# The long sequence's gates as a stage of block products between Fourier mixing and retention, the short sequence's gates as filler

## The chip, the cores and the metric

The kernel runs on one core of one Trainium2 chip. The metric is the device time of one execution in microseconds (us); of several runs the median is given. The chip has a matrix engine (TensorE, PE in the profile, with its weight loads as PEld), VectorE (DVE), ScalarE (ACT), GpSimd (POOL), and SyncE (SP), whose queue issues most of the transfers between the device's memory (HBM) and the on-chip memory. Products accumulate in eight banks (`bank`) that DVE and ACT read out.

## The reference

One encoder layer with the same weights over two requests, one of 512 tokens and one of 1024, model width 1024:

```python
u = rms_norm(x, norm1_g)
f, q, k, v, g_ret, g_a, g_b = split(u @ w_in)       # 512, 512, 512, 1024, 1024, 1024, 1024 columns
branch_a = fourier_mix(f) @ w_four_proj             # 4 groups of 128: fft2 over tokens and channels, real part
branch_b = (group_norm(bidirectional_retention(q, k, v)) * silu(g_ret)) @ w_ret_proj
x = x + (sigmoid(g_a) * branch_a + sigmoid(g_b) * branch_b) @ w_out
x = x + (gelu(conv3(h_gate)) * h_val) @ w_down      # h_gate, h_val = split(rms_norm(x, norm2_g) @ w_up), 2816 each
y = rms_norm(x, final_norm_g)
```

Retention has 8 heads (keys of 64, values of 128), runs in chunks of 128 tokens in both directions with a decay per head, and rotates q and k.

## The kernel before

**Layout.** Activations lie with the channels on the 128 partitions: tile `x[t, k]` holds channels 128k to 128k+127 (k = 0 to 7) of 512 tokens. t=0 is the short sequence, t=1 and t=2 the long one. Every float32 product is made of three matmuls of rounded halves (`mm3`, L110 to L112): high by high, low by high, high by low. `split` makes the halves: ACT copies the high one (L74), DVE subtracts for the low one (L75). `slab` (L93) loads 128x1024 weights through SP into `wr` and splits them into `wh` and `wl`. A projection of 128 output channels and 512 tokens takes 24 matmuls of 128x512 (`proj_steps`).

**The norm.** `Prep` loads x (`fetch`, L187), makes u = x * g as halves (`scale`, L195 on ACT, L196 on DVE), without 1/rms. Squares come from ACT or POOL (`SumSq`); `cols` sums them over the partitions on PE (L130), DVE adds (L133), POOL raises to the power -1/2 (L134); `rows` spreads that over the partitions for a row per token (`rrow`). The factor is applied later: by `rrow` on the gates, per token on the Fourier channel DFT (L255, L256) and on q, k, v (L530). So no projection waits for the norm.

**Stages.** (1) Projection of f for t=0, 1, 2 (`f_proj`) with `channel_dft` (L249) and `sequence_dft` of the short sequence between; (2) channel and sequence DFT of the long one; (3) a loop over 8 output blocks n that multiplies the Fourier result `pq` with `w_four_proj`, then makes gate g_a of the three t (`gate`, L310: times `rrow` on DVE, sigmoid on ACT), multiplies it with the branch (L491) and stores the result (`ma`, L492); (4) retention over four head pairs: per pair 12 chunks of q, k, v (128 tokens by 512 columns, 24 matmuls each), then six g_ret gates of 24 matmuls, each with one POOL product (L683), while `sides` do the chunks' other steps on PE's gaps, the states and group norm (`ret_states`, L624 to L635) and the multiplication with g_ret (`ret_store`); (5) gates g_b for n=1 to 7 (`gb_main`), beside which the last pair's side work and the splitting of retention's results run; n=0 has run as a filler in the long sequence DFT; (6) merge (g_a part plus g_b times retention's projection), `w_out`, the up and down projections and the last norm. The stages from the merge on already compute pairs of 512-token halves as 2x2 blocks with seven products in place of eight (`w_ops`, `quad`, `quads`): a job is 7 products of 12 matmuls, 84.

**Order.** Code order gives each instruction's rank on its engine, and every engine and every queue runs in its order; an instruction waits for the semaphores of what it needs and for the space of its output. SP waits with a transfer for its source or its destination, and what is behind it waits too. The tiles u live from the norm to the last g_b gate. Line numbers here are those of the profile before.

Of the kernel before, what the change touches and what calls it, by code (L numbers as in the profile page):

```python
# [14 lines left out]
P = 128  # L15
# [9 lines left out]
SL_F, SL_GA, SL_GRET, SL_QKV, SL_GB = 0, 4, 12, 20, 36  # L25
SL_RP, SL_WO, SL_DL = 44, 52, 60
N_SLABS = 62
# [8 lines left out]
def emit(ctx, tc, x, wsl, wup, wdq, wd0, wfour, tab, cst, rcst, vec, out):  # L36
# [4 lines left out]
    uctx, wctx = ExitStack(), ExitStack()  # L41
    upool = uctx.enter_context(tc.tile_pool(name="u", bufs=24))
# [25 lines left out]
    x2_d = [[spill(f"xx{n}_{t}") for t in range(3)] for n in range(KD)]  # L68

    def utile(kind, dtype=F32R):  # L70
        return upool.tile([P, TC], dtype, name=kind, tag=kind)
# [5 lines left out]
    state = {"ww": (1152, 1032)}  # L77
# [5 lines left out]
    def wtiles():  # L83
        wpool = state["w"]
        wide, cols = state["ww"]
        r = wpool.tile([P, wide], F32, name="wr", tag="wr", bufs=2)
        state["turn"] += 1
        pool, n = (state["wx"], 1) if state["wx"] and state["turn"] % 5 == 4 or state["turn"] < 0 else (wpool, 4)
        return (r, *(pool.tile([P, cols], F32R, name=x, tag=x, bufs=n) for x in ("wl", "wh")))
# [70 lines left out]
    state["w"] = wctx.enter_context(tc.tile_pool(name="w", bufs=4, reuse_waits="tile"))  # L160
    bctx = ExitStack()
    rc = bctx.enter_context(tc.tile_pool(name="rc", bufs=1, reuse_waits="tile"))
    state.update(wx=bctx.enter_context(tc.tile_pool(name="wx", bufs=1, reuse_waits="tile")), turn=-1)

    fctx = ExitStack()
    pqp = fctx.enter_context(tc.tile_pool(name="pq", bufs=1, side="right", reuse_waits="tile"))
    f1ctx = ExitStack()
    fp = f1ctx.enter_context(tc.tile_pool(name="f1", bufs=13, side="right", reuse_waits="tile"))

    state["tmp"] = fp, "f2", 13  # L170
    u = [None] * 3
    rcol, rrow = [None] * 3, [None] * 3

    class Prep:
        def __init__(self, t):
            self.t = t
            self.ss = SumSq(rc.tile([P, R_END], F32, name="rs", tag="rs")[:, :TC] if t == 0 else None, t == 2)
            self.xs = []
            u[t] = ([], [])
# [10 lines left out]
        def scale(self):  # L190
            k = len(u[self.t][0])
            xs = self.xs[k]
            g = vc[:, V_G1 + k:V_G1 + k + 1]
            h, l = utile("uh"), utile("ul")
            nc.scalar.activation(h, xs, AF.Identity, scale=g)  # L195
            nc.vector.scalar_tensor_tensor(l, xs, g, h.bitcast(F32), op0=ALU.mult, op1=ALU.subtract)  # L196
            u[self.t][0].append(h)
            u[self.t][1].append(l)

        def square(self, k):  # L200
            self.ss.add(self.xs[k], self.t == 1 and k % 2 == 1)
            self.xs[k] = None
# [4 lines left out]
        def rows(self):  # L207
            ps = rstd_rows(rcol[self.t])
            rrow[self.t] = rc.tile([P, TC], F32, name=f"rrow{self.t}")
            nc.scalar.copy(rrow[self.t], ps)  # L210

# [24 lines left out]
    def channel_dft(si, pr):  # L236
        c0, ncs, t0, nt = SEQS[si]
        zt = []
        for c2 in range(ncs // 2):
# [11 lines left out]
            for j in range(2):  # L251
                c = 2 * c2 + j
                b = slice(j * 256, (j + 1) * 256)
                r = rcol[t0 + c // 4][:, c % 4:c % 4 + 1]
# [53 lines left out]
    def gate(pool, tag, ps, t, bufs=None):  # L308
        sg = pool.tile([P, TC], F32, name="sg", tag=tag, bufs=bufs)
        nc.vector.tensor_tensor(sg, ps, rrow[t], op=ALU.mult)  # L310
        nc.scalar.activation(sg, sg, AF.Sigmoid)
        return sg

    def gb_main(ns, pool, tag, bufs=None):
        for n in ns:
            wgb = wslab(SL_GB + n)
            for t in range(3):
                ps = bank()
                for _ in proj_steps(ps, wgb, u[t]):
                    yield  # L320
                sg = gate(pool, tag, ps, t, bufs)
                nc.scalar.dma_start(sb_d[n][t], sg)
                yield

# [3 lines left out]
    for k in range(4):  # L328
# [3 lines left out]
        preps[0].scale()  # L332
# [5 lines left out]
    for k in range(4):  # L338
        preps[0].scale()
# [3 lines left out]
    for k in range(KD):  # L343
        preps[0].square(k)
    fps = [bank() for _ in range(4)]
# [3 lines left out]
    preps[0].cols()  # L349
    for g in range(4):  # L350
        f_evac(0, g, fps[g])
    for k in range(KD):
        preps[1].scale()
        preps[1].square(k)

# [11 lines left out]
    for k in range(KD):  # L367
        preps[2].fetch()
    f_proj(1, 0)
    z00 = channel_dft(0, 0)  # L370
    f_proj(1, 1)
    z01 = channel_dft(0, 1)
    preps[1].cols()
    for k in range(KD):
        preps[2].scale()
    for i, _ in enumerate(sequence_dft(0, {0: z00, 1: z01})):
        preps[2].square(2 * i)
        preps[2].square(2 * i + 1)
    f_proj(2, 0)
# [10 lines left out]
    f_proj(2, 1)  # L390
    preps[2].cols()
# [17 lines left out]
    rs = rc.tile([P, R_END], F32, name="rs", tag="rs")  # L409
    nc.sync.dma_start(rs, rcst)  # L410

    decD, decT = {}, {}

    def decay_d(hp):
        D = rc.tile([P, 2, P], F32, name="D", tag="D", bufs=4)
# [11 lines left out]
    def decay_t(hp):  # L427
        TD = rc.tile([P, 2, P], F32, name="TD", tag="TD", bufs=2)
# [10 lines left out]
    for hp in range(4):  # L439
        decay_d(hp)  # L440
# [4 lines left out]
    state["turn"] = -1  # L445
    for q in preps:
        q.rows()
    z11 = channel_dft(1, 1)
    fill = gb_main(range(1), fp, "f2", 13)
    next(fill)  # L450
    for _ in sequence_dft(1, {1: z11}):
        next(fill, None)
    list(fill)
    f1ctx.close()

# [869 lines left out]
```

## Time and profile before

| | |
|---|---|
| runs: median (lowest to highest), us | 2282.02 (2279.92 to 2282.39), 3 runs |
| profiled execution, us | 2279.94 |
| its span, us | 2277.8 |
| busy in the span: PE, DVE, ACT, POOL | 98%, 65%, 37%, 15% |
| mean granted clock of PE | 0.991 |
| moved by DMA | 273.30 MB, 120 GB/s on the mean |

The profile is of one execution, whose own time is 2.1 us longer than its span. A row of a stretch gives for each engine its busy time in it, with the count of instructions, then PE's granted clock, the share of time that the DMA engines were busy, and what they moved. A row of a group gives line, engine, operation, output and inputs, count, then busy time, mean ns of one, and the idle time just ahead of it with what ended that. In a row of the timeline stand start, duration and the instruction, and in brackets how long the engine had been idle and what released it.

### The profile page before, as it was taken

Reading aid. Unit: us, or ns where it says so; the run is one execution under the profiler, and the core shown is the slowest. Engines: PE = TensorE matmul, PEld = TensorE weight load, DVE = VectorE, ACT = ScalarE, POOL = GpSimd, SP = SyncE. Lnnn points to the kernel's source line nnn. Section 1 sums busy time; section 2 is a strip of 40 time slices with the busy share of each in tenths; the row PEclk is TensorE's granted clock in tenths of the full one; section 3 lists DMA queues with packets and bytes.
Section 4 is the critical chain, followed back from the end, with each engine's and each line's share of the span. In section 5 each row is a group of like instructions: output and inputs, shape, how many; then the busy total and the mean of one; then the engine's idle time right before and its main releaser. Section 6 shows DMA issues by size and latency. Waiting matters only on the chain. (4 is left out here: it accounts for less than half of the span.)

```text
span 2277.8 us, 29367 instructions
## 1 busy us (share of the span) xinstructions
PE 2228.0 (98%) x11294; PEld 1866.6 (82%) x11294; DVE 1474.6 (65%) x2555; ACT 848.5 (37%) x1373; POOL 345.8 (15%) x184
## 2 busy tenths in 40 slices
PE   8899999999999999999999999999989999999997
PEld 6788888888888888878887788888867878999986
DVE  7453434656556462255678886767689888999744
ACT  6251222223121221133334444434453446666413
POOL 2799601111212120010120000000000000000001
PEclk9999999999999999999999999999999999999999
DMA  5252220111102012276756452323265455333462
GB/s 190 66 167 86 94 84 1 47 38 38 47 17 68 1 56 79 74 243 224 226 180 226 147 191 94 110 93 116 84 226 176 153 203 195 101 104 112 166 208 70
DMA packets 103531, 273.30 MB, mean 120 GB/s; under 512 B 11488, under 2 KB 14816, under 8 KB 97760
## 3 DMA queue, kind: packets, MB, share of 16 engines
q1 hardware_dynamic: 99936, 265.15, 35.1%
q10 hardware_dynamic: 3456, 6.29, 0.7%
q8 instruction: 88, 1.44, 0.3%
q14 instruction: 51, 0.42, 0.1%
HBM read 208.22 MB, written 63.18 MB: 119 GB/s over the span
## 5 line engine op out<-in xcount | busy, mean ns | idle before, releaser
L110 PE MATMUL bank<-op,wh 128*128 128x512 f32 (+1 forms) x1320 | 462.0, 352 | 8.0 <-DVE y L1096 4.2
L111 PE MATMUL bank<-op,wl 128*128 128x512 f32 (+1 forms) x1320 | 463.2, 351 | 1.1 <-DVE wl L75 1.1
L112 PE MATMUL bank<-op,wh 128*128 128x512 f32 (+1 forms) x1320 | 461.6, 350 | 1.1 <-DVE op L75 1.1
L75 DVE TENSOR_TENSOR wl<-wr,wh 128x1024 fp32r<-128x1024 f32 (+5 forms) x210 | 250.3, 1193 | 163.5 <-ACT wh L74 161.7
L74 ACT CAST wh<-wr 128x1024 fp32r<-128x1024 f32 (+5 forms) x210 | 204.8, 977 | 325.1 <-PE bank L112 220.7
L110 PEld LDWEIGHTS bank<-op,wh 128*128 128x128 f32 x1320 | 250.0, 189 | 48.3 <-DVE y L1096 5.2
L112 PEld LDWEIGHTS bank<-op,wh 128*128 128x128 f32 x1320 | 250.4, 190 | 37.6 <-DVE op L75 2.0
L111 PEld LDWEIGHTS bank<-op,wl 128*128 128x128 f32 x1320 | 250.3, 190 | 36.4 <-DVE wl L75 1.6
L110 PE MATMUL bank<-uh,wh 128*128 128x512 f32 x672 | 271.5, 404 | 5.2 <-ACT wh L74 5.2
L112 PE MATMUL bank<-ul,wh 128*128 128x512 f32 x672 | 266.0, 396 | 0.0
L111 PE MATMUL bank<-uh,wl 128*128 128x512 f32 x672 | 265.9, 396 | 0.0
L134 POOL TENSOR_TENSOR nr<-nv,mhalf 128x4 f32<-128x4 f32 (+1 forms) x10 | 12.9, 1285 | 1105.7 <-DVE nv L133 1075.8
L425 POOL TENSOR_TENSOR D<-two,D 128x64 f32<-128x64 f32 x16 | 170.2, 10667 | 0.0
L74 ACT CAST wh<-wt 128x1024 fp32r<-128x1024 f32 (+2 forms) x120 | 117.3, 977 | 135.9 <-PE bank L112 123.9
L110 PE MATMUL bank<-wh,uh 128*128 128x512 f32 x384 | 166.6, 434 | 0.0
L110 PEld LDWEIGHTS bank<-uh,wh 128*128 128x128 f32 x672 | 126.8, 189 | 32.1 <-ACT wh L74 5.2
L111 PE MATMUL bank<-wh,ul 128*128 128x512 f32 x384 | 151.4, 394 | 0.0
L112 PE MATMUL bank<-wl,uh 128*128 128x512 f32 x384 | 151.0, 393 | 0.0
L112 PEld LDWEIGHTS bank<-ul,wh 128*128 128x128 f32 x672 | 126.6, 188 | 29.4
L111 PEld LDWEIGHTS bank<-uh,wl 128*128 128x128 f32 x672 | 126.8, 189 | 27.7 <-DVE wl L75 0.8
L310 DVE TENSOR_TENSOR sg<-bank,rrow 128x512 f32<-128x512 f32 x48 | 33.2, 691 | 165.5 <-PE bank L112 165.5
L75 DVE TENSOR_TENSOR wl<-wt,wh 128x1024 fp32r<-128x1024 f32 (+2 forms) x120 | 135.6, 1130 | 6.5 <-ACT wh L74 6.3
(233 smaller groups left out, 4108.5 us busy)
## 6 DMA issues: line engine op xcount, KB each, us to landing
wr<-wsl SPq DMA_DIRECT2D x92, 512.0 KB, 3.9
wr<-wup SPq DMA_DIRECT2D x44, 1024.0 KB, 4.9
xs<-x SPq DMA_DIRECT2D x48, 256.0 KB, 4.2
wr<-tab SPq DMA_DIRECT2D x18, 516.0 KB, 3.7
wr<-wdq SPq DMA_DIRECT2D x12, 768.0 KB, 4.2
wr<-wd SPq DMA_DIRECT2D x16, 512.0 KB, 3.9
sb<-sg ACTq DMA_DIRECT2D x24, 256.0 KB, 2.0
ma<-sg SPq DMA_DIRECT2D x24, 256.0 KB, 2.0
```

The costliest lines, as they stand in the source:

```text
L74: nc.scalar.copy(h, src)
L75: nc.vector.tensor_tensor(l, src, h.bitcast(F32), op=ALU.subtract)
L110: nc.tensor.matmul(o, lh, rh, start=first, stop=False, skip_group_check=go_on)
L111: nc.tensor.matmul(o, ll, rh, start=False, stop=False, skip_group_check=go_on)
L112: nc.tensor.matmul(o, lh, rl, start=False, stop=last, skip_group_check=go_on)
L134: nc.gpsimd.tensor_tensor(r, v, mhalf[:, 0:n], op=ALU.pow)
L310: nc.vector.tensor_tensor(sg, ps, rrow[t], op=ALU.mult)
L425: nc.gpsimd.tensor_tensor(D[:, m], two.broadcast_to([P, 64]), D[:, m], op=ALU.pow)
```

## The change

**The long sequence's gates.** The three gates of t=1 and t=2 become 12 block jobs (`gate_job`) of 84 matmuls, run by the same `quads` that the up stage uses, in a stage of their own between Fourier and retention: 1008 matmuls in place of 1152. Eight jobs give g_a and g_b for n, four give g_ret for two n. Each loads 128x2048 weights (`wg`) and, for the first eight, the branch.
- The jobs need four sums of the operands u (S1 to S4, k = 0 to 3). `sums` makes them on DVE in the front, splits them and stores them in HBM (`s_d`); 32 loads of 256 KB bring them back (`sop`) at the gate stage's start. The branch of t=1, 2 is stored too (`br_d`, 8 x 512 KB), and the finished gates go to HBM.
- Sums need operands of one scale, so u of t=1 and t=2 is now normalised in `scale`: x * g * rrow on DVE, then split. Their rstd is therefore needed ahead of their f projection. All squares are ACT's.
- All of u of t=0 (`u0_d`) and a part of t=2 (`a21_d`) are stored by `keep` on SP's queue as they are made, and loaded again ahead of retention.
- The decay tables (`decay_d`, POOL) move from the Fourier stages into the gate stage.

**The short sequence's gates** stay plain (24 matmuls). `first_gates` makes g_ret as filler in the front, in the sequence DFTs and in the projection loop, g_a in that loop, g_b 0 and 1 ahead of the gate stage, g_b 2 to 7 after retention.

**Retention** takes the long sequence first, has no gates of its own on PE, and loads g_ret (`sg`) in `ret_states`, which now also calls `ret_store`.

The core of the diff:

```diff
     class Prep:
...
-        def scale(self):
+        def scale(self, k):
...
+            if self.t:
+                nc.vector.scalar_tensor_tensor(xs, xs, g, rrow[self.t], op0=ALU.mult, op1=ALU.mult)
+                split(h, l, xs)
+                if self.t == 2 and k < 4:
+                    keep((h, l), a21_d[k])
+            else:
+                nc.scalar.activation(h, xs, AF.Identity, scale=g)
+                nc.vector.scalar_tensor_tensor(l, xs, g, h.bitcast(F32), op0=ALU.mult, op1=ALU.subtract)
+                keep((h, l), u0_d[k])
...
+    def sums(k):
...
+        s2 = tmp("s2")
+        nc.vector.tensor_tensor(s2, a21, a22, op=ALU.add)
+        put("S1", s2)
+        nc.vector.tensor_tensor(a21, a11, a21, op=ALU.subtract)
+        put("S3", a21)
...
     for k in range(KD):
-        preps[1].scale()
+        preps[2].fetch()
+    for k in range(KD):
         preps[1].square(k)
+    preps[1].cols()
+    preps[1].rows()
+    for _ in range(6):
+        next(fill)
+    for k in range(KD):
+        preps[1].scale(k)
+    for k in range(KD):
+        preps[2].square(k)
+    preps[2].cols()
+    preps[2].rows()
+    f_proj(1, 0)
+    f_proj(1, 1)
...
-        for t in range(3):
-            sg = gate(f2, "sga", proj(wga, u[t]), t)
-            nc.vector.tensor_tensor(sg, sg, br[:, t * TC:(t + 1) * TC], op=ALU.mult)
-            nc.sync.dma_start(ma_d[n][t], sg)
+        sg = gate(proj(wga, u[0]))
...
+        nc.sync.dma_start(ma_d[n][0], sg)
+        nc.sync.dma_start(br_d[n], br[:, TC:])
...
+    sop = right("sop", 32, g2ctx)
...
+                nc.sync.dma_start(o.bitcast(F32), d)
...
+    for _ in first_gates("gb", range(2)):
+        pass
...
+    nc.sync.dma_start(rs, rcst)
+    for hp in range(4):
+        decay_d(hp)
...
+        return lambda: w_ops(wg[i], 512), uop, TC, pair_sink(g, v, TC), done
+
+    for _ in quads(gate_job(i) for i in range(12)):
+        pass
```

**Where instructions go.** SP's queue at the start, before: x tiles (`xs`) and weights (`wr`) alternate.

```order
L187 DMA xs<-x 128x512
L102 DMA wr<-wsl 128x256 x2
L187 DMA xs<-x 128x512 x4
L93 DMA wr<-wsl 128x1024 x2
L187 DMA xs<-x 128x512 x8
```

The same queue after, from the second x tile on (`u0h`, `u0l` are the halves of u of t=0 on their way to HBM):

```order
L308 DMA xs<-x 128x512
L107 DMA wr<-wsl 128x256 x2
L294 DMA u0h_234<-u 128x512
L294 DMA u0l_235<-u 128x512
L294 DMA u0h_236<-u 128x512
L294 DMA u0l_237<-u 128x512
L308 DMA xs<-x 128x512
L107 DMA wr<-wsl 128x256 x2
```

Four stores, which wait for their u, have come ahead of the third and fourth x tile, and twelve more ahead of the later ones.

PE behind the f projection of t=0, before (`ones,rs` are the sums of squares of t=0, the rows after them the f projection of t=1):

```order
L112 MATMUL bank<-ul,wh 128x512
L130 MATMUL bank<-ones,rs 128x1 x4
L110 MATMUL bank<-uh,wh 128x512
L111 MATMUL bank<-uh,wl 128x512
L112 MATMUL bank<-ul,wh 128x512
```

After (two norms, of t=0 and of t=1, each with its rows, then the filler):

```order
L117 MATMUL bank<-u,wh 128x512
L135 MATMUL bank<-ones,sq 128x1 x4
L145 MATMUL bank<-cs,nr 128x128 x4
L135 MATMUL bank<-ones,sq 128x1 x4
L145 MATMUL bank<-cs,nr 128x128 x4
L115 MATMUL bank<-u,wh 128x512
```

The squares of t=1 have moved ahead of everything that PE does next; those of t=2 stand 48 matmuls further on, ahead of the f projection of t=1.

SP's queue behind the projection loop, before (the last stores of g_a times branch, then weights of retention):

```order
L492 DMA ma_0_98<-sg 128x512
L492 DMA ma_1_99<-sg 128x512
L93 DMA wr<-wsl 128x1024
L492 DMA ma_2_100<-sg 128x512
L93 DMA wr<-wsl 128x1024 x4
```

After (`s` are the operand sums, `rs` constants, `b` the branch, `wr_3068` the first block job's weights):

```order
L659 DMA br_201<-br 128x1024
L658 DMA ma_0_95<-sg 128x512
L676 DMA s<-S1h_202 128x512
L676 DMA s<-S1l_203 128x512
...
L676 DMA s<-S4l_233 128x512
L688 DMA rs<-rcst 128x1024
L700 DMA b<-br_194 128x1024
L173 DMA wr_3068<-wg 128x2048
```

The 32 loads of the sums stand between the store of the last g_a and the first block job's weights; on PE, n=7's g_a and two g_b gates, 72 matmuls, stand between the last Fourier product and the first block job.

More of the change, by code (lines that the diff above doesn't have):

```diff
@@ new lines, in emit, with tick, quads @@
+    late = []
+    def tick():
+        for it in list(late):
+            if next(it, late) is late:
+                late.remove(it)
+    def quads(jobs):
+        prev = None
+        for prep, act, cols, sink, after in jobs:
+            w = prep()
+            g = quad(w, act, cols, sink)
+            next(g)
+            if prev:
+                next(prev[0])
+                prev[1]()
+                tick()
+            next(g)
+            tick()
+            prev = g, after
+            yield
+        next(prev[0])
+        prev[1]()
+        tick()
@@ L612, in ret_states @@
         for q in range(nt):
+            sg = [rp.tile([P, TC], F32, name="sg", tag="sg", bufs=4) for _ in range(2)]
+            for i in range(2):
+                nc.sync.dma_start(sg[i], gr_d[2 * hp + i][t0 + q])
             st = rp.tile([P, 4, 2, 6], F32, name="st", tag="st")
```

449 lines of the change are left out of this document (247 added, 202 removed).

## The prediction

> **What bounds the kernel now.** I read the page's totals first, then the stretches in which TensorE (PE) falls short, then the rows of those stretches. First the page: span, PE's and VectorE's (DVE) totals, and two rows of its DMA table.
>
> ```profile
> span 2277.8 us, 29367 instructions
> PE 2228.0 (98%) x11294; PEld 1866.6 (82%) x11294; DVE 1474.6 (65%) x2555; ACT 848.5 (37%) x1373; POOL 345.8 (15%) x184
> wr<-wup SPq DMA_DIRECT2D x44, 1024.0 KB, 4.9
> xs<-x SPq DMA_DIRECT2D x48, 256.0 KB, 4.2
> ```
>
> PE is busy 2228.0 of 2277.8 us: a matmul taken away is worth its pitch, and only 49.8 us of idle are there to win. What decides is whether the new order makes PE wait. Next the busy time by stretch (PE, PEld, DVE, ACT, POOL, clock, DMA share, GB/s).
>
> ```profile
> 12.00:25.00 13.00, 13.00 (x58) 10.42 (x57) 10.18 (x15) 11.29 (x18) 0.00 (x0) 1.00 0.97 348
> 40.00:60.00 20.00, 12.96 (x80) 10.97 (x78) 19.73 (x40) 6.46 (x12) 11.09 (x11) 0.91 0.09 27
> 60.00:80.00 20.00, 14.89 (x62) 12.09 (x63) 8.26 (x10) 3.68 (x8) 8.47 (x7) 0.74 0.18 53
> 177.00:338.00 161.00, 161.00 (x828) 136.54 (x827) 66.93 (x117) 35.55 (x59) 86.21 (x11) 1.00 0.27 85
> 426.00:556.00 130.00, 129.12 (x663) 107.46 (x662) 74.35 (x225) 31.63 (x72) 23.05 (x25) 1.00 0.12 37
> 966.00:976.00 10.00, 6.20 (x25) 4.32 (x23) 2.60 (x3) 2.31 (x3) 0.00 (x0) 0.95 0.56 173
> 976.00:986.00 10.00, 9.95 (x31) 7.87 (x32) 3.14 (x3) 2.09 (x2) 0.84 (x1) 0.71 0.80 295
> ```
>
> Projection (177 on) and a retention head pair (426:556) are full of PE. Idle lies in the front (7.04 and 5.11 us in two rows) and at the merge (3.80). The first row is what saturated DMA gives: share .97, 348 GB/s.
>
> **1. Fewer products: −33.6.** The long sequence's three gates were 8 x 2 x 3 groups of 24 matmuls, 1152; now 12 jobs of 84, 1008. Pitches: the evictions of four neighbouring gates (first and last), and the first evictions of the up stage's jobs of the same form.
>
> ```profile
> 954.79 0.69 DVE L310 TENSOR_TENSOR sg<-bank,rrow 128x512 f32<-128x512 f32 x1 [4.90 <-PE bank L112]
> 971.59 0.69 DVE L310 TENSOR_TENSOR sg<-bank,rrow 128x512 f32<-128x512 f32 x1 [4.91 <-PE bank L112]
> L943 ACT COPY g<-bank x5: 586/586/587, 1408.7 to 1486.9; 128x512 f32<-128x512 f32 x5
> ```
>
> 16.80 / 72 = 0.2333 us a matmul; (1486.9 − 1408.7) / 4 = 19.55 a job, 0.2327 each. So 12 x 19.55 = 234.6 against 268.8: −34.2; I take 144 x 0.2333 = −33.6. DVE and ScalarE (ACT) work of a job, some 10 and 8 us, fits beside it, and POOL's decay powers, moved here, fit into the stage:
>
> ```profile
> L425 POOL TENSOR_TENSOR D<-two,D 128x64 f32<-128x64 f32 x16 | 170.2, 10667 | 0.0
> ```
>
> **2. Front: +10.8.** Rows of the sync queue (SP), DVE, ACT and PE:
>
> ```profile
> 2.58 0.43 SPq L187 DMA_DIRECT2D xs<-x  x1
> 7.60 0.75 DVE L196 SCALAR_TENSOR_TENSOR ul<-xs,vc,uh 128x512 fp32r<-128x512 f32 x1 [0.80 <-ACT uh L195]
> 16.20 1.05 ACT L74 CAST wh<-wr 128x1024 fp32r<-128x1024 f32 x1 [0.95 <-DMA wr<-wsl]
> 20.89 3.74 ACT L153 ACTIVATE sq<-xs 128x512 f32<-128x512 f32 x7
> 29.52 0.95 PE L130 MATMUL bank<-ones,rs 128*128 128x1 f32 x8
> 81.97 0.95 PE L130 MATMUL bank<-ones,sq 128*128 128x1 f32 x8
> 82.78 2.48 PE L249 MATMUL bank<-cs,ft 128*128 128x128 f32 x20
> 83.02 0.16 DVE L133 TENSOR_SCALAR nv<-bank 128x4 f32<-128x4 f32 x1 [10.31 <-PE bank L130]
> 83.26 1.02 POOL L134 TENSOR_TENSOR nr<-nv,mhalf 128x4 f32<-128x4 f32 x1 [14.71 <-DVE nv L133]
> ```
>
> The new stores of u stand in SP's queue ahead of the loads of x tiles 2 and 3, and wait for DVE's split of tile 1 (7.60 + 0.75 = 8.35); those loads went out from 2.58. So the rest of the front load is 5.9 later: cast 22.1, first projection done 29.5 + 5.9 = 35.4. The long sequence now needs its rstd before its projection: four copies (2.4), eight squares at 3.74 / 7 = 0.53 with the last add (5.0), the chain above (81.97 to 84.3, and some 1 us for its rows), 46; PE idles nearly all of it. 48 filler matmuls (11.2, and 1.7 for a cold clock) last to 59, then PE waits again, for t=2's squares behind sixteen splits on ACT and DVE: 69.6. With two projections, the short channel and sequence DFT and 33 filler matmuls, PE reaches the long channel DFT at about 112.5. Before it was 82.78; the 81 matmuls brought forward are 18.9, so 101.7 would be no loss: +10.8. The squares no longer on POOL are a gain within this: DVE stood beside POOL's work at 40:60 (DVE 19.73 of 20, POOL 11.09). Bounds: 0 (all of it hidden by that gain) to +17 (the front's own idle again).
>
> **3. Before the long sequence DFT: +5.** The operand sums of k=2 and 3, 16 to 18 DVE operations of 0.7 (11 to 13 us), stand ahead of the evictions that the channel DFT needs. Cover is the filler; 0 to +10.
>
> **4. Projection: 0.** Per n DVE had 66.93 of 161, and its rest and the stores fit.
>
> **5. Start of the gate stage: +28, the term that decides.** SP issues 32 loads of the operand sums (8.39 MB), the constants (0.5), the branch (0.5) and the first job's weights (1.05), 10.5 MB, in this order, behind the store that needs n=7's gate. That gate ends 7.8 us after the last Fourier product (24 matmuls 5.6, three operations of about 0.7). At 348 GB/s 10.5 MB take 30.1, landing takes some 2 more: weights at 40. ACT's and DVE's splits take
>
> ```profile
> L75 DVE TENSOR_TENSOR wl<-wr,wh 128x1024 fp32r<-128x1024 f32 x30 | 37.4, 1246 | 11.6 <-ACT wh L74 11.5
> L74 ACT CAST wh<-wr 128x1024 fp32r<-128x1024 f32 x30 | 31.5, 1049 | 49.8 <-PE bank L112 21.8 <-issue 9.9 <-DMA wr<-wsl 8.1
> 974.79 0.65 PE L110 MATMUL bank<-gh,wh 128*128 128x512 f32 x1 [3.24 <-ACT wh L74]
> ```
>
> 1.05 before the first matmul, 1.25 before the second. PE's cover is n=7's gate and two g_b gates, 72 matmuls, 16.8. Stall 41.3 − 16.8 = 24.5, second matmul 1.2, cold clock. The last row is PE's first matmul after such a wait: in 976:986 the clock was 0.71, so 2.9 us went in ten; I take 2.3. Bounds: the loads hidden, yet constants, branch and weights (2.1 MB, 6 us, plus 2.3 and 1.7) still wait for u's space, free only when PE's cover ends: +10; a rate of 295 GB/s (976:986) gives 35.6 for the load: +34.
>
> The Trainium skill ("DMA: Bandwidth & Descriptors", Where 436 GB/s comes from) holds two ceilings against each other: about 358 GB/s by the HBM, and 425 measured for one large transfer with the pair's other core idle. This trace's .97 share at 348 GB/s speaks for the first. By 425 the load would take an estimated 24.7 us instead of 30.1, and this term +23. The Trainium skill ("TensorE: Matmul & The Clock Gate", Part 1) has PE at half clock after an idle window of about 3.4 us until it was busy as long, an estimated 1.7 lost; the row with 0.71 agrees in kind and shows more.
>
> **6. Retention: +3 and +4.5.** A head pair keeps its 288 projection matmuls and loses 144 (33.6): 129.12 becomes about 96, and DVE 74.35 less its gate work, about 68, 70%. Latency, which gates hid, can show; I take 3 for four pairs (0 to 16: from nothing to 4 a pair). At the end the last group norm,
>
> ```profile
> L628 POOL TENSOR_TENSOR rr<-rr,mhalf 128x8 f32<-128x8 f32 x7 | 12.1, 1734 | 24.3 <-DVE rr L627 24.1
> L624 DVE BATCH_NORM_STATS2 st<-o 128x6 f32<-128x128 f32 x58 | 14.0, 283 | 0.5
> L635 DVE TENSOR_SCALAR o<-o,mv,rr 128x128 f32<-128x128 f32 x56 | 16.1, 354 | 11.0 <-POOL rr L628 11.0
> L622 DVE TENSOR_TENSOR o<-bank,o 128x256 f32<-128x256 f32 x30 | 12.7, 422 | 20.5 <-PE bank L621 20.2
> ```
>
> an add 0.42, two heads' statistics some 0.9, two small operations and crossings some 0.8, the power 1.73, two scalings 0.70, stands before the transposes with nothing of PE's between: +4.5 (0 to 6). Before, g_b's gates lay there.
>
> **7. Merge: −6.5.** Before, every u tile lived to the last gate, and the merge's first slab waited: 3.80 idle and 2.9 of clock. After, its space is over the long sequence's u, free since retention, and three gates (16.8) cover load and split. Bounds −6.5 to 0.
>
> **Sum:** −33.6 + 10.8 + 5 + 28 + 3 + 4.5 − 6.5 = +11.2. The profiled execution took 2279.94, its span and 2.1 around it; the median of the runs, 2282.02, is 2.1 above. So 2279.94 + 11.2 + 2.1 = 2293.2.
>
> **Rivals.**
> A. Faster: the operand sums arrive in time, or do not hold the weights up, so term 5 costs its lower bound, 10, not 28, and front and sums cost half (8 of 15.8): 2293 − 18 − 8 = 2267. It decides if the first job's weights land within about 25 us of the last Fourier product. For it: DMA share is only .27 in projection; against it: one queue, and the loads stand ahead of the weights.
> B. About as before: term 5 as said, but the front costs nothing (POOL's squares were the stall) and retention no latency: 2293 − 10.8 − 3 = 2279.
> C. Retention becomes DVE's: 4 us or more a head pair, and the gates' filler is missed: 2293 + 13 to 2306. For it: DVE 70%, a long chain through POOL; against: DVE 74.35 of 130 with 0.88 of PE idle so far.
> D. Block jobs slower than plain gates, so that the 144 matmuls bring nothing: +34, 2327. The up stage's 19.55 a job speaks against it.
>
> By the higher DMA ceiling of the Trainium skill's page "DMA: Bandwidth & Descriptors" the time would be an estimated 2288, inside the likeliest case.
>
> **Chances.** Forecast (2284 to 2302) 0.5; A 0.2; B 0.14; C 0.13; D 0.03. The range 2266 to 2306 reaches A's and C's values. Of ±0.2%, ±4.5 us and about what a measurement here tells from no change: faster is A and a third of B (0.25), same is the rest of B and the forecast's lower edge (0.15), slower the rest (0.60).
>
> **What would show it.** Right: PE idle of 20 us or more just before the first block job, released by a weight cast that waited for its DMA, at full DMA share; PE idle twice in the first 70 us, released by rstd; a job's pitch of 19.55; a retention pair near 97; no wait at the merge. Wrong: weights landing during the g_b gates, a front that reaches the long channel DFT before 105, or a retention pair above 100.

## The result, and the profile after

The changed kernel took 2347.28 us (median of 4 runs, 2345.24 to 2349.09), the kernel before 2281.73 on the same chip: a ratio of 1.0288, interval 1.0271 to 1.0306. It is 65.6 us slower; 11 slower was predicted, with a range that ended at 2306. The medians of two kernels below leave out one run each that took more than twice as long (7424.61 us with the later stores, 5825.69 us with three edits together). The head of the page, before: 2277.8 us, PE 2228.0.

```profile
span 2343.5 us, 29601 instructions
PE 2214.2 (94%) x11150; PEld 1851.6 (79%) x11150; DVE 1573.7 (67%) x2690; ACT 925.3 (39%) x1473; POOL 288.9 (12%) x141
```

The products did go: 144 fewer matmuls. But PE is busy only 13.8 us less, not 33.6, and its idle time has risen from 49.8 to 129.3 us, by 79.5. The sum, −13.8 + 79.5 = +65.7, is the spans' difference. Where the idle lies is seen by stretch (PE, PEld, DVE, ACT, POOL, granted clock, DMA share, GB/s):

```profile
40.00:80.00 40.00, 18.82 (x80) 15.80 (x80) 27.12 (x39) 20.93 (x32) 2.73 (x2) 0.72 0.28 93
80.00:120.00 40.00, 30.07 (x149) 25.40 (x148) 23.55 (x61) 11.54 (x21) 10.95 (x4) 0.88 0.28 105
120.00:160.00 40.00, 29.41 (x149) 24.19 (x150) 27.86 (x56) 18.95 (x37) 0.00 (x0) 0.80 0.64 218
320.00:360.00 40.00, 13.08 (x55) 9.89 (x53) 8.93 (x26) 3.70 (x6) 4.65 (x1) 0.72 0.86 314
360.00:596.00 236.00, 235.53 (x1006) 190.29 (x1006) 123.67 (x136) 95.00 (x118) 167.53 (x19) 0.99 0.36 115
680.00:720.00 40.00, 37.23 (x209) 31.50 (x208) 33.16 (x112) 10.44 (x26) 7.00 (x9) 1.00 0.28 86
```

Three stretches of the first 160 us lose 41.7 us of PE, the start of the gate stage (320:360) 26.9. The gate stage itself (360:596) is full. The clock is low just where PE waited, so the matmuls that follow a wait are slow too. Retention (680:720) is nearly full, and yet loses: its waits are short and many. The waits by name, from PE's timeline (start, duration, instruction, and in brackets the idle time and its releaser):

```profile
24.33 1.22 PE L115 MATMUL bank<-u,wh 128*128 128x512 f32 x2 [5.62 <-ACT wh L79]
50.53 0.80 PE L145 MATMUL bank<-cs,nr 128*128 128x128 f32 x2 [2.36 <-POOL nr L139]
78.21 1.87 PE L135 MATMUL bank<-ones,sq 128*128 128x1 f32 x8 [13.67 <-DVE sq L162]
125.52 0.58 PE L115 MATMUL bank<-wh,zh 128*128 128x258 f32 x1 [14.04 <-ACT zh L404]
142.61 0.60 PE L395 MATMUL bank<-cs,ft 128*128 128x128 f32 x3
154.50 0.80 PE L115 MATMUL bank<-wh,zh 128*128 128x258 f32 x2 [4.56 <-ACT zh L79]
359.29 0.80 PE L115 MATMUL bank<-u,wh 128*128 128x512 f32 x1 [26.92 <-ACT wh L79]
684.45 0.70 PE L808 MATMUL bank<-qbd,kT 128*128 128x256 f32 x2 [1.27 <-DVE qbd L803]
983.50 0.70 PE L808 MATMUL bank<-qbd,kT 128*128 128x256 f32 x2 [1.31 <-DVE qbd L803]
1014.46 0.70 PE L890 MATMUL bank<-cs,o 128*128 128x128 f32 x2 [4.70 <-DVE o L879]
1037.77 0.80 PE L115 MATMUL bank<-gh,wh 128*128 128x512 f32 x1 [2.89 <-ACT wh L79]
```

The first projection waits for weights whose loads stand behind the stores of u (the row at 24.33); no such wait was there before. The norms of t=1 and t=2 end late (the rows at 50.53 and 78.21). Then comes a wait that the prediction did not have: 14.04 us before the short sequence's DFT. The long channel DFT starts at 142.61; 101.7 would have been no loss. The wait of 26.92 at the gate stage's start is the one that the prediction called decisive. In retention the waits for `qbd` come back in each head pair.

### The profile page after: what moved, and what is told of

Read it like the earlier page. It is cut to its first block, busy times and chain, and to the rows that moved or that the text cites. A ratio compares the mean times of both kernels' runs of the same rounds, so it can differ in the third digit from the quotient of the medians.

```text
span 2343.5 us, 29601 instructions
## 1 busy us (share of the span) xinstructions
PE 2214.2 (94%) x11150; PEld 1851.6 (79%) x11150; DVE 1573.7 (67%) x2690; ACT 925.3 (39%) x1473; POOL 288.9 (12%) x141
## 5 line engine op out<-in xcount | busy, mean ns | idle before, releaser
L80 DVE TENSOR_TENSOR wl<-wr,wh 128x1024 fp32r<-128x1024 f32 (+5 forms) x222 | 263.3, 1187 | 205.1 <-ACT wh L79 203.2
L79 ACT CAST wh<-wt 128x1024 fp32r<-128x1024 f32 (+2 forms) x144 | 142.5, 989 | 181.2 <-PE bank L117 170.3
L115 PE MATMUL bank<-u,wh 128*128 128x512 f32 x432 | 176.9, 410 | 37.4 <-ACT wh L79 37.4
L116 PE MATMUL bank<-u,wl 128*128 128x512 f32 x432 | 175.3, 406 | 1.6 <-DVE wl L80 1.5
L117 PE MATMUL bank<-u,wh 128*128 128x512 f32 x432 | 174.7, 404 | 0.0
L80 DVE TENSOR_TENSOR wl<-wt,wh 128x1024 fp32r<-128x1024 f32 (+2 forms) x144 | 164.9, 1145 | 11.0 <-ACT wh L79 10.8
L115 PE MATMUL bank<-wh,u 128*128 128x512 f32 x384 | 166.7, 434 | 0.0
L116 PE MATMUL bank<-wh,u 128*128 128x512 f32 x384 | 151.4, 394 | 0.0
L117 PE MATMUL bank<-wl,u 128*128 128x512 f32 x384 | 150.9, 393 | 0.0
L115 PEld LDWEIGHTS bank<-u,wh 128*128 128x128 f32 x432 | 84.6, 196 | 56.5 <-ACT wh L79 38.3
L116 PEld LDWEIGHTS bank<-u,wl 128*128 128x128 f32 x432 | 84.2, 195 | 22.9 <-DVE wl L80 3.9
L117 PEld LDWEIGHTS bank<-u,wh 128*128 128x128 f32 x432 | 83.6, 194 | 19.5
L117 PEld LDWEIGHTS bank<-wl,u 128*128 128x128 f32 x384 | 72.1, 188 | 16.9
```

Source lines behind the costliest of these rows:

```text
L79: nc.scalar.copy(h, src)
L80: nc.vector.tensor_tensor(l, src, h.bitcast(F32), op=ALU.subtract)
L115: nc.tensor.matmul(o, lh, rh, start=first, stop=False, skip_group_check=go_on)
L116: nc.tensor.matmul(o, ll, rh, start=False, stop=False, skip_group_check=go_on)
L117: nc.tensor.matmul(o, lh, rl, start=False, stop=last, skip_group_check=go_on)
```

## The experiments

The theory after the result: the loss is four separate stalls (front, gate stage's start, retention, end of retention), each from an order on an engine or queue or from missing space, and none from the block products. The rival for each is that another engine or transfer stands at that place and the time stays. Where one edit changes one cause, its gain is given against 2347.28; the kernel before, run beside each of them, had medians of 2281.3 to 2282.3, so a difference of 1 us tells nothing. Each `next(fill)` makes one third of a filler gate, 8 matmuls.

### Front: the stores of u of t=0 behind the loads of x

```diff
-                keep((h, l), u0_d[k])
...
     for k in range(KD):
+        keep((u[0][0][k], u[0][1][k]), u0_d[k])
+    for k in range(KD):
         preps[1].square(k)
```

> Only the 16 stores of u of t=0 are issued later on SP's queue, behind the loads of x of t=1 and t=2. Theory (queue order): the third and fourth x tile go out from about 5 us instead of 8.2, the second weight cast of the first projection starts near 17 instead of 23.2, and the whole front comes 5 to 7 us earlier: 2340 to 2342. Rival (ACT and DVE bound the front: squares, normalising, splits): what PE gains at the first projection it waits longer for the norm of t=1, the long sequence's channel DFT still starts near 142, 2346 to 2348.

2348.11 us, 1.0287 (1.027 to 1.0304): no gain. PE's timeline in this kernel:

```profile
42.20 2.07 PE L145 MATMUL bank<-cs,nr 128*128 128x128 f32 x8 [1.42 <-POOL nr L139]
51.19 0.79 PE L115 MATMUL bank<-u,wh 128*128 128x512 f32 x1 [6.91 <-ACT wh L79]
78.19 1.86 PE L135 MATMUL bank<-ones,sq 128*128 128x1 f32 x8 [11.86 <-DVE sq L162]
```

The first step of the prediction's front was true: without the stores the norm of t=1 comes 8.3 us sooner (42.20 for 50.53), where 5.9 had been put down for them. But PE then waits 6.91 for the filler's weights, and the norm of t=2 comes at the same 78.2. What sets that norm is not the load.

### Front: the projection of t=1 ahead of the norm of t=2

```diff
-    preps[2].cols()
-    preps[2].rows()
     f_proj(1, 0)
     f_proj(1, 1)
+    preps[2].cols()
+    preps[2].rows()
```

> Only PE's order changes: the first two f projections of t=1 stand ahead of the norm of t=2, not behind it. Theory (order): the idle time of 13.67 us ahead of t=2's sums falls under 4, as u of t=1 is split by 70, and the long channel DFT starts 8 to 13 us sooner: 2334 to 2339. Rival (ACT and DVE bound the front): the rows of t=2's norm come no sooner, u of t=2 is split no sooner, PE waits the same time later, at t=2's projection: gain under 4 us.

2336.73 us, 1.0234 (1.0216 to 1.0252): 10.6 gained. PE's timeline:

```profile
78.32 1.02 PE L135 MATMUL bank<-ones,sq 128*128 128x1 f32 x8 [2.30 <-DVE sq L162]
115.55 0.58 PE L115 MATMUL bank<-wh,zh 128*128 128x258 f32 x1 [14.05 <-ACT zh L404]
```

The norm of t=2 stands at 78.3 for the third time, so it is set by DVE and ACT; now PE has work until then (13.67 to 2.30 idle). The second wait is unchanged. In the changed kernel's trace, ACT's rows show what the norm of t=2 is behind:

```profile
66.97 0.63 ACT L477 ACTIVATE g<-sg 128x512 f32<-128x512 f32 x1 [0.78 <-DVE sg L463]
67.50 0.61 ACT L158 ACTIVATE sq<-xs 128x512 f32<-128x512 f32 x1
73.62 1.15 ACT L158 ACTIVATE sq<-xs 128x512 f32<-128x512 f32 x2 [1.99 <-DMA gr<-sg]
```

Its first square starts at 67.50, behind the splits of u of t=1 and behind the filler gates' own activations and weight splits, and at 73.62 a square waits 1.99 us for space that the store of a filler's gate gives back. By these rows the filler that was to cover the norm delays it; no run left the filler out.

### Front: two more tiles of space

`NF = 15` becomes `NF = 17` in the front's pool of working tiles.

> Only the pool of the front's work tiles grows from 15 to 17. Theory: DVE's last eviction of the first channel DFT waited 8.7 us for space, and the operand sums of k=0 and 1 behind it; with space they run beside PE's projection of t=2 and the 14.04 us of idle before the short sequence DFT falls to 4 to 8: 2337 to 2341. Rival: the sums themselves (16 operations of 0.69, with waits for stores) are the wait; the idle stays at 12 or more, 2346 or more.

2340.93 us, 1.0255 (1.0238 to 1.0272): 6.4 gained. PE's timeline:

```profile
75.78 1.87 PE L135 MATMUL bank<-ones,sq 128*128 128x1 f32 x8 [10.82 <-DVE sq L162]
120.56 0.58 PE L115 MATMUL bank<-wh,zh 128*128 128x258 f32 x1 [10.15 <-ACT zh L404]
```

Both waits fall by some 3 to 4 us; the 10.15 left of the second lies between what the theory and the rival gave. Why it exists, DVE's rows of the changed kernel show:

```profile
109.85 0.48 DVE L405 SCALAR_TENSOR_TENSOR zl<-bank,nr,zh 128x256 fp32r<-128x256 f32 x1 [8.71 <-PE bank L395]
110.25 0.68 DVE L349 TENSOR_TENSOR s<-xs 128x512 f32<-128x512 f32 x1
116.28 0.69 DVE L80 TENSOR_TENSOR sx<-s,sx 128x512 fp32r<-128x512 f32 x1 [1.42 <-DMA S3h<-sx]
125.50 0.48 DVE L405 SCALAR_TENSOR_TENSOR zl<-bank,nr,zh 128x256 fp32r<-128x256 f32 x1 [1.03 <-ACT zh L404]
```

From 110.25 to 124.5 the operand sums of k=0 and 1 (L349 to L355 with their splits) stand on DVE ahead of the evictions of the short sequence's second channel DFT (L405 at 125.50); one of them waits for the store of an earlier sum to give back its tile. ACT casts for the same sums, and its share of that eviction (L404), which PE waits for, stands behind them. Nor could the sums start sooner: DVE first stood idle for 8.71 us, until PE's second channel DFT (L395, from 108.09), so that none of them ran beside PE's projection of t=2. With two tiles more, DVE's first sum starts at 98.50, but ACT's cast for it then waits 10.39 us for the same matmuls. So two tiles more let only the first two operations of the sums through.

### Front: filler around the norms

This kernel put filler before and after each norm, gave the squares a place of their own and set two or three thirds of a filler gate behind each of the four sums.

> The front in another order, with the same instructions: two and two thirds of the short sequence's g_ret gates cover the norms of t=1 and t=2, squares of t=2 stand ahead of the normalising of t=1 and have their own space, projections go tile by tile, and seven gates' thirds stand beside the operand sums. Theory (order, not ACT's and DVE's amount of work, made the 40.9 us): the idle before the norm of t=2, before the short and the long sequence DFT fall together from 13.7 + 14.0 + 4.6 to under 10, and the norm of t=1 costs under 3: 2312 to 2325. Rival (DVE's amount): DVE is busy 95% from 45 to 130 us and PE still waits 20 or more: 2330 or more.

2341.26 us, 1.0262 (1.0244 to 1.0279): 6 gained, no more. It also has the 17 tiles and another order of squares and projections. The waits for the two norms fell to 2.30 and 3.96, but the sums began only at 118.73, behind PE's second channel DFT (116.31) and the splits of the filler's weights, and the wait before the short sequence's DFT was 15.85 us at 135.54. The cover stood ahead of the sums, not beside them.

### Front: the three edits and filler where DVE has the sums

```diff
+    NF = 17
...
     z01 = channel_dft(0, 1)
+    for _ in range(6):
+        next(fill)
     for _ in sequence_dft(0, {0: z00, 1: z01}):
...
         sums(k)
+    for _ in range(4):
+        next(fill)
```

with the stores behind the first filler gates' loads and the projection of t=1 ahead of the norm of t=2, as above.

> The front once more, with what the runs before showed: the stores of u of t=0 behind the filler's weights, t=1's first projections ahead of the norm of t=2, 17 work tiles, and six thirds of the short sequence's g_ret gates on PE just where it waited for the operand sums of k=0 and 1, four more where it waits for those of k=2 and 3. Theory (order and space; PE's filler must stand where DVE works the sums off): 10.6 of the earlier projections, 6 of the earlier start, 8 to 10 of the cover add up: 2318 to 2326. Rival (each wait only moves to the next place, as with the later stores alone): 2332 or more.

2317.53 us, 1.0158 (1.0139 to 1.0176): 29.8 gained. Alone, the three edits had given nothing, 10.6 and 6.4; the filler was not run alone, so its share is only what is left, some 13. PE's timeline:

```profile
39.95 1.87 PE L135 MATMUL bank<-ones,sq 128*128 128x1 f32 x8 [5.91 <-DVE sq L162]
107.40 0.58 PE L115 MATMUL bank<-wh,zh 128*128 128x258 f32 x1 [3.11 <-ACT zh L403]
```

The waits of 13.67 and 14.04 are gone but for 3.11, and that before the long sequence's DFT, 4.56, has fallen below 1. The longest wait left in the front is that of the norm of t=1, 5.91; the gate stage's start now waits 27.96, 1.0 more than in the changed kernel.

### Gate stage: weights ahead of half the sums

The first job's weights are requested behind S1 and S2, and S3, S4, the constants and the branch behind them.

```diff
+    s_load("S1")
+    s_load("S2")
...
+            w = w_ops(wg[i], 512)
+            if i == 0:
+                s_load("S3")
+                s_load("S4")
+                nc.sync.dma_start(rs, rcst)
```

> At the gate stage's start the sums S1 and S2 are loaded first, then the first job's weights, then S3, S4, constants and branch. Theory: the weights stood behind 10 MB in one queue; they now land about 25 us after the last Fourier product instead of 40, the idle of 26.9 falls to 9 to 13, and S3 and S4 come in time: 2331 to 2335. Rival: the first job needs all sums anyway, it starts earlier and stops inside for S3 and S4, so that less than 5 us is won.

2330.44 us, 1.0214 (1.0199 to 1.0229): 16.8 gained; the wait falls from 26.92 to 11.35:

```profile
344.31 0.80 PE L115 MATMUL bank<-u,wh 128*128 128x512 f32 x1 [11.35 <-ACT wh L79]
```

### Gate stage: weights first, on space that is free

The first two jobs' weights get tiles that do not lie over u (the g_b gates before them have two tiles in place of four), the first job's load is coded ahead of all sums, and the store of the last g_a, which SP waited for, goes out on ACT's queue.

```diff
+                nc.sync.dma_start(given[0]["raw"], wg[0])
+                for name in ("S1", "S2", "S3", "S4"):
...
-        nc.sync.dma_start(ma_d[n][0], sg)
+        (nc.scalar if n == 7 else nc.sync).dma_start(ma_d[n][0], sg)
```

> The first block job's weights get space that is free before the last gates (in place of u of the short sequence), their load stands ahead of S3 and S4, and the last store of g_a goes to ACT's queue, so that SP's loads of the sums start with the last Fourier product. Theory (queue order and space were the whole wait): the weights land before PE's 16.8 us of cover end, S4 comes by 29 us where PE needs it at 31; of the idle 26.9 at most 4 stay: 2320 to 2326. Rival (DMA bound: 10 MB take 30 us whatever their order): PE waits inside the first job instead, 10 us or more stay, 2330 or more.

2326.11 us, 1.0198 (1.0183 to 1.0213): 21.2 gained.

```profile
338.52 0.80 PE L115 MATMUL bank<-u,wh 128*128 128x512 f32 x1 [5.87 <-ACT wh L79]
```

5.87 us stay: on SP's queue the weights still came behind 13 loads of the sums, since the order of the code is not alone what sets the queue's order, and SP stood still for some 5 us ahead of the seventh of them. By the releasers in SP's rows, that load waited 5.2 us for the store of the last g_a, which ACT's queue had sent off at 323.60, and a load of S3 later waited 7.6 us for the store of a g_b gate. So the store no longer stood in SP's queue, yet a load there still waited for it. In the changed kernel a load of S3 waited 3.9 us in the same way.

### Retention: filler gates into the head pairs

Three of the g_b gates that came after retention run inside its first three pairs.

```diff
+                    yield from first_gates("gb", [2 + hp])
...
-    drive(first_gates("gb", range(2, 5)))
```

> Three of the short sequence's g_b gates (24 matmuls each) move from behind retention into the first three head pairs, after the long sequence's chunks; the count of instructions is the same. Theory (retention lost 15 us because PE's other work, the gates, is gone and DVE's waits show): the pairs that have a gate lose 1.5 to 3 us less each, 2338 to 2344. Rival (the waits lie early in the chunks, before the gate's place, or the cover is missed behind retention as much as it helps inside): 2345 to 2350.

2349.32 us, 1.0302 (1.0287 to 1.0317): no gain, as the rival had it. PE's timeline, one wait inside and one at the end:

```profile
711.22 0.70 PE L808 MATMUL bank<-qbd,kT 128*128 128x256 f32 x2 [1.72 <-DVE qbd L803]
1021.65 0.70 PE L890 MATMUL bank<-cs,o 128*128 128x128 f32 x2 [4.06 <-DVE o L879]
```

More PE work in the pairs does not help where PE stands in order behind one copy; the waits only change place: those for `qbd` come to 10.8 us where they were 12.1, and the end of retention waits 3.53 and 4.06 where it waited 4.70.

### Retention: the copy to ACT

```diff
-        nc.vector.tensor_copy(qbd[64:128, 1], tp[64:128, P:2 * P])
+        nc.scalar.copy(qbd[64:128, 1], tp[64:128, P:2 * P])
```

> One copy of 64x128 per chunk, for which PE waits in retention, goes from DVE (0.29 us) to ACT, 48 in all. Theory (DVE is full where the states and group norm of the pair before run beside chunks, 33 of 40 us at 680:720): PE's waits for this copy shrink, 4 to 9 us are won, 2338 to 2343. Rival (latency of the chain, whichever engine does the step): within 2 us of 2347.

2337.15 us, 1.0249 (1.0234 to 1.0265): 10.1 gained. The longest of these waits inside retention is now

```profile
984.02 0.70 PE L808 MATMUL bank<-qbd,kT 128*128 128x256 f32 x2 [1.12 <-ACT qbd L803]
```

and the next are 0.60 to 0.71. In the changed kernel the copy's line stands with this row among those who waited for it (us, times):

```profile
  PE bank L808: 12.1, 13
```

So 12.1 us of PE were lost there. With the copy on ACT the same row has 5.3 us in 11 waits, 6.8 less; 10.1 were gained in all, and PE's busy time, too, fell by 4.8 us (2209.4 for 2214.2). Why the copy was late, DVE's rows ahead of one of these waits say:

```profile
679.99 1.40 DVE L879 TENSOR_SCALAR o<-o,mv,rr 128x128 f32<-128x128 f32 x4 [1.33 <-POOL rr L872]
681.84 1.10 DVE L879 TENSOR_SCALAR o<-o,mv,rr 128x128 f32<-128x128 f32 x4
682.86 1.21 DVE L80 TENSOR_TENSOR wl<-wr,wh 128x1024 fp32r<-128x1024 f32 x1
684.10 0.29 DVE L803 COPY qbd<-bank 64x128 f32<-64x128 f32 x1
```

A copy of 0.29 us stands behind eight scalings of the group norm, two updates of the state (between them, not shown) and a split of weights, 4.1 us of work for which PE was not waiting.

### Retention: is it DVE's load, or the burst?

One theory was that DVE is too full (33.16 of 40 us in 680:720): then taking the scalings off DVE gains what taking the copy off gained. The other was that the burst ahead of the copies does it, on whatever engine. Two kernels move the scalings to ACT (bias and scale in one activation): one with the copies on ACT as well, one with the copies left on DVE.

```diff
+            nc.vector.scalar_tensor_tensor(nb, mv.rearrange("p j i s -> p (j i) s")[:, :, 0], -1.0, rr,
+                                           op0=ALU.mult, op1=ALU.mult)
...
-                    nc.vector.tensor_scalar(os[c][:, m], os[c][:, m], mv[:, j, i, 0:1],
-                                            rr[:, 2 * j + i:2 * j + i + 1], op0=ALU.subtract, op1=ALU.mult)
+                    nc.scalar.activation(os[c][:, m], os[c][:, m], AF.Identity, bias=nb[:, 2 * j + i:2 * j + i + 1],
+                                         scale=rr[:, 2 * j + i:2 * j + i + 1])
```

Both on ACT:

> With the copy on ACT, the group norm's scaling of 128x128 (0.35 us, 96 in all) also goes from DVE to ACT, as scale and bias; one small DVE operation is added per group. Theory (DVE's load beside the chunks): what is left of retention's loss after the copy's move, some 5 us, shrinks by 2 to 4: 2333 to 2335. Rival (what is left is the chain's latency; ACT 25% busy, but the steps are no shorter there): 2336 to 2339.

2347.65 us, 1.0288 (1.0267 to 1.031): the 10.1 us of the copies' move are lost again.

Scalings alone on ACT:

> From the changed kernel alone: the group norm's scaling goes to ACT, the copy that PE waits for stays on DVE (before, both moved: 2347.65; the copy alone: 2337.15). Theory (the copy waits in its engine's queue behind the burst of group norm, so the two must stand on different engines, whichever does what): 2336 to 2341, like the copy alone. Rival (DVE's load, of which the scaling is the larger part, or the scaling's own latency on ACT): 2345 or more if ACT's latency sets it, under 2334 if it is DVE's load.

2347.15 us, 1.0285 (1.027 to 1.0301): no gain. ACT's and then PE's row of this kernel at the same place as above:

```profile
682.40 2.04 ACT L882 ACTIVATE o<-o,nb,rr 128x128 f32<-128x128 f32 x5 [1.98 <-DVE nb L876]
686.02 0.26 ACT L802 COPY qbd<-bank 64x128 f32<-64x128 f32 x1
```

```profile
686.67 0.70 PE L808 MATMUL bank<-qbd,kT 128*128 128x256 f32 x2 [1.69 <-DVE qbd L803]
```

The first half of `qbd` is copied by ACT (L802), so the burst now delays that half, the copy on DVE waits 2.31 us for it, idle, and PE waits 1.69. The kernel that gained nothing has DVE busy for 28.32 of the 40 us in 680:720, the one that gained 10.1 us for 32.98. So the load of DVE is not the reason; the place in the queue is. The theory's 2336 to 2341 was missed, since one half of the copy stands on ACT from the start.

### End of retention: one gate more as cover

```diff
-    drive(first_gates("gb", range(2, 5)))
+    drive(first_gates("gb", range(2, 6)))
```

> From the changed kernel alone: g_b gate 5 stands ahead of the closing of retention's space and the merge's loads, so that four gates and not three lie beside the last pair's side work. Theory (the 4.70 us of idle before the last transposes, and the cold clock behind it, came from too little PE work there): 5 to 8 won, 2339 to 2342. Rival (the gate is missed where the merge's operands are loaded): the idle before the merge grows, 2345 or more.

2340.26 us, 1.0258 (1.0244 to 1.0272): 7.0 gained. The 4.70 at the end is gone, but the merge, which lost that gate as its cover, waits longer:

```profile
1034.92 0.80 PE L115 MATMUL bank<-gh,wh 128*128 128x512 f32 x1 [4.96 <-ACT wh L79]
```

That is 2.07 more of waiting for 4.70 less, which alone would be a gain of 2.6; the rest, some 4, is in PE's busy time (2209.4 for 2214.2): by the granted clock PE was busy 52.0 us at half clock in the changed kernel and 44.1 here, and half of the difference makes an estimated 4 us.

### All together

The front of 29.8, the weights first and the copies on ACT in one kernel:

> front4, the first job's weights on free space and the copy on ACT together. Theory (the three losses are of different stages and add up: 25 + 21 + 10): 2287 to 2295. Rival (they overlap: an earlier front makes the gate stage's transfers meet others): 2298 or more.

2284.78 us, 1.002 (1.0008 to 1.0033): 62.5 gained, where the three alone gave 29.8 + 21.2 + 10.1 = 61.1. With the scalings on ACT and the tail as well:

> best2 with the group norm's scaling on ACT too and one more g_b gate ahead of the merge's loads, so that the last pair's side work has PE work beside it. Theory: 2 to 4 us of retention and 2 to 4 of the 4.7 at its end are won: 2280 to 2290, about the kernel before. Rival (the gate is missed where the merge's operands are split): the idle before the merge grows by as much, 2290 or more.

2286.62 us, 1.0024 (1.0012 to 1.0035): no further gain. With the tail, and the scalings left on DVE:

> The front as in the last form, first weights on free space, the copy on ACT with the scaling left on DVE, and the gate moved at the end. Theory (losses of different stages add up): 2286.3 less 5 to 9: 2277 to 2282. Rival (they overlap): 2284 or more.

2282.13 us, 1.0006 (0.9997 to 1.0014). Last, the same with a filler gate ahead of the sums of squares of t=1:

> The same with the first filler gate ahead of the norm of t=1, where PE idled 5.91 + 2.36 us and ran cold behind it. Theory (the long sequence's norm, which the sums need, costs nothing where a gate stands beside it): 4 to 8 less than the run without, 2271 to 2277. Rival (the gate's split and eviction delay the squares): no gain, within 2 of it.

2283.51 us, 1.0006 (0.9997 to 1.0015): the waits of that norm went, others of 2.66 and 3.41 us took their place.

So the edits at the four places add up: alone they give 29.8 + 21.2 + 10.1 + 7.0 = 68.1, together 65.2. That this is about the 65.6 that had been lost is chance: with the 33.6 us of products saved, the new order had cost 99.2, and some 34 of that remain. No version is measurably faster than the kernel before. The page and three of PE's waits of the third kernel:

```profile
PE 2206.7 (97%) x11150; PEld 1848.4 (81%) x11150; DVE 1552.5 (68%) x2642; ACT 936.6 (41%) x1521; POOL 289.4 (13%) x141
```

```profile
38.84 1.44 PE L135 MATMUL bank<-ones,sq 128*128 128x1 f32 x6 [5.91 <-DVE sq L162]
307.84 0.80 PE L115 MATMUL bank<-u,wh 128*128 128x512 f32 x1 [6.96 <-ACT wh L79]
972.88 0.80 PE L115 MATMUL bank<-gh,wh 128*128 128x512 f32 x1 [6.13 <-ACT wh L79]
```

Its span is 2281.1. PE is busy 21.3 less than before (12.3 of the 33.6 went to slower matmuls), and idle 74.4 instead of 49.8: the products saved are spent on these waits and small ones. Whether an order exists without them stays open.

## Why the prediction was wrong

The direction was right, the time 54 us too low, and outside the range. By its own terms, as measured from stage to stage in the two traces:

| term | predicted | measured |
|---|---|---|
| 1 products | −33.6 | −33.6 by the count of matmuls; the stage of 12 jobs took 237.3 instead of 234.6 |
| 2 front | +10.8 (0 to 17) | +40.9 |
| 3 before the long sequence's DFT | +5 | +7.0, 4.56 of it in one wait |
| 4 projection | 0 | inside term 3's figure |
| 5 gate stage's start | +28 (10 to 34) | 26.92 idle, 29.6 with the slow matmuls |
| 6 retention, and its end | +3 and +4.5 | 14.4 and 4.70 |
| 7 merge | −6.5 | −0.4 in the wait, +2.7 behind it |

**Term 2 is the step that failed.** It had PE reach the long channel DFT at about 112.5; it was 142.61. The sums of k=0 and 1, which stand on DVE ahead of the channel DFT's second eviction, were not in it at all: I had priced those of k=2 and 3, in term 3, by the same reasoning, and passed over the first two. That is 14.04 us, shown by the rows at 109.85 to 125.50 and by the last kernel of the front, which has filler there. None of it ran beside the projection of t=2, since DVE waited 8.71 us ahead of the sums for PE's second channel DFT. The norm of t=2 was put at 69.6 as "t=2's squares behind sixteen splits on ACT and DVE"; its rows came at 81.49. The first projection, too, was done later, at 38.5 and not 35.4 (the 5.9 of its shift is 8.35 − 2.58 = 5.8, and 9.0 were measured), but by the kernel with the later stores this is not what sets the norm of t=2. The filler gates' activations, weight splits and stores stand in the same two queues, and I had counted the filler as PE work only. Of the 30.1 us between 112.5 and 142.61 the sums (14.0) and the late norm (11.9) make 25.9; the other 4.2 lie between 81.49 and 142.61, where the granted clock was 0.86 on the mean. The upper bound of 17 was the idle of the front before, which bounds nothing that the change adds.

**Term 6.** Rival C was right in kind and was kept out of the sum. A pair's pitch is (983.50 − 684.45) / 3 = 99.7, where 130 − 33.6 = 96.4 was the forecast: 3.3 a pair, and 12.1 us of waits for one copy. The reason given for C, DVE's share of 70%, was not the reason; the burst is. The price for C, 4 a pair, was near. The end of retention, +4.5, came out as 4.70, released by the group norm's scaling as worked out.

**Term 7.** I had looked at the space and the load of the merge's first slab, and both were free in time. I had not looked at ACT's order:

```profile
1035.65 0.63 ACT L481 ACTIVATE sg<-sg 128x512 f32<-128x512 f32 x1 [2.10 <-DVE sg L463]
1036.68 1.04 ACT L79 CAST wh<-wr 128x1024 fp32r<-128x1024 f32 x1 [0.40 <-ACT sg L481]
```

The slab's cast stands behind the sigmoid of the last g_b gate, which can run only once that gate's matmuls are done. The wait before the merge is 2.89, against 3.24 before: 0.4 gained, and the rest of the kernel behind it is 2.7 us longer in all, not traced further. So the step "three gates (16.8) cover load and split" held for the load and failed for the split.

**What held.** Term 5, the largest, was right in place, mechanism and size: from SP's rows, the store that needs n=7's gate went out at 323.31, the weights' request behind the 32 loads at 349.71, and ACT's cast waited for them until 358.19:

```profile
323.31 0.32 SPq L658 DMA_DIRECT2D ma<-sg  x1
349.71 0.33 SPq L173 DMA_DIRECT2D wr<-wg  x1
```

```profile
358.19 1.04 ACT L79 CAST wh<-wr 128x1024 fp32r<-128x1024 f32 x1 [24.43 <-DMA wr<-wg]
```

The DMA moved 314 GB/s at a share of 0.86 there, with SP's stop of 3.9 us in it; 348 at 0.97 was the basis. The prediction took 348 for what saturated DMA gives, and that was too low: the changed kernel moved 393 GB/s from 25 to 40 us and 406 from 346 to 358. The Trainium skill ("DMA: Bandwidth & Descriptors", Where 436 GB/s comes from) has about 358 for the HBM's side and 425 as measured for one large transfer. The trace passes the first and does not reach the second. Rivals A and B fell with this term and with term 2; D fell with the 237.3 us.

## What to carry to other kernels

When a change moves work, write down for each engine what stands in its queue ahead of the operation that the critical engine will wait for, and price every piece of it, the filler's own evictions, activations and stores too: here 14 us lay in sums, 12 in a burst ahead of a copy of 0.29 us, and 2.9 in one cast behind a sigmoid. Filler covers a stall only where it is placed, and its own evictions lengthen the queues of the engines whose delay it is meant to cover. A saving on an engine that was busy 98% of the time is worth its pitch only as long as the new order keeps it at 98%: bound each new stall by what is queued ahead, not by the idle time that the old order had.

## What the runs showed of the hardware that was not expected

- **A wait is paid twice, the second time by the clock.** PE's busy time fell by 13.8 where 33.6 us of matmuls were removed, so 19.8 us went to slower ones. By the granted clock PE was busy 52.0 us at half clock, and 21.7 in the kernel before; half of the difference makes an estimated 15.2 us of the 19.8, and the rest was not traced. After the wait of 26.92 matmuls started 0.43 us apart (361.14, 361.57) instead of 0.233:

```profile
361.14 0.63 PE L117 MATMUL bank<-u,wh 128*128 128x512 f32 x1
361.57 0.63 PE L115 MATMUL bank<-u,wh 128*128 128x512 f32 x1
```

  The Trainium skill ("TensorE: Matmul & The Clock Gate", Part 1) has PE at half clock until it has been busy for a window of about 3.4 us, an estimated 1.7 us each time. The trace agrees in the ratio (0.43 to 0.233), but the changed kernel has 13 waits of over 2.3 us and the one before seven; six more would make an estimated 10 us by that figure, where the granted clock gives 15.2.
- **A store can hold up a computation.** ACT and DVE waited 1.99 and 1.42 us for stores of a filler's gate and of a sum, since these tiles are free only when the store has read them. Two more tiles were worth 6.4 us.
